# Where a two-level weight product takes its block sums from: sums that grow in place in DRAM, another order of v's seven products, and v's weights split in halves

## The chip, the cores and the metric

The kernel runs on one core of one Trainium2 chip. The metric is device time in microseconds (us) of one execution. Five engines work from queues of their own: TensorE (PE, matrix products), VectorE (DVE), ScalarE (ACT), GpSimd (POOL) and SyncE (SP, which here only issues DMAs). POOL issues DMAs too, and the copies with an addition that this text is about are all POOL's.

## The reference

One layer on x (512 tokens, 2048 channels), float32. What matters here are two of its products:

```python
h = _rmsnorm(x, g_pre)
proj = h @ w_in                       # q | k | v | z_att | u | g_glu | z_conv, 1024 columns each
q, k, v, z_att, u, g_glu, z_conv = jnp.split(proj, IN_SPLITS, axis=-1)
y_att = _stick_breaking_attention(q, k, v) * jax.nn.silu(z_att)
y_conv = _conformer_conv(u, g_glu, conv_w, conv_b, ln_g, ln_b, w_pw2, b_pw2) * jax.nn.silu(z_conv)
y = jnp.concatenate([y_att, y_conv], axis=-1) @ w_out
out = x + _rmsnorm(y, g_post)
```

## The kernel before

Every float32 operand of a product is split in two parts of a shorter type: `hi` on ACT and `lo` = source minus `hi` on DVE (`split`, L96). A product is then three matmuls (hi·hi, hi·lo, lo·hi).

The program is a list of steps. A step loads one 1 MB block of weights (SP, into a `raw` buffer), splits it, and runs two units on PE. For q, k, u and the gates a step is half of the 2048 rows of 256 columns: 48 matmuls. For v a step is 24 matmuls. `raws`, `his` and `los` have two buffers each. So the load for a step can start when the split of the step two before it has ended, and a split can start when PE has left the `hi` and `lo` of the step two before it.

Two of the products, v (L532 to L649) and the output projection (L831 to L972), use a scheme with seven products in place of eight. The weight matrix is cut into 2 x 2 blocks (r, c). Products 1, 3 and 2 use a plain block, products 5, 6, 7 and 4 a sum of blocks, and seven "forms" of the activations (sums and differences of blocks of h, made by `make_v_form` on DVE and split on ACT and DVE) stand on the other side. Sum 5 is (0,0)+(0,1), sum 6 is sum 5 + (1,1), sum 4 is sum 6 + (1,0), sum 7 is (0,1)+(1,1). Each block and sum has two halves by rows, kg 0 and 1; below, "5.0" is product 5, half 0, and so on. v has 14 such steps of one pair, w_out 28 of two pairs.

The sums are made in DRAM by POOL's DMA queue (`plan_sums`, L492): a copy of the base (L506), then a copy of another block that is added to it (L502, `accum_op`). Both are put in a queue, `v_sumq` or `sumq`, and `sum_next` (L514) takes the next one at fixed places of the program: one behind each of the later blocks of the first stage, then one behind each unit of a step (v), or one per step from step 18 on (w_out). `sum_next` makes the DMA wait for the last matmul issued so far by the functions that record it (`latest`).

In v the order of products is `V_ORDER = (1, 2, 5, 6, 3, 7, 4)`. The forms are made when a certain step's weights are loaded: `{(1, 0): 5, (2, 1): 6, (6, 1): 3, (3, 0): 7}` (L614). Instructions carry priorities. PE keeps the order of the program text; ACT, DVE, POOL and SP get a fixed order in which the scheduler placed them by priority. Between v's splits on DVE stand the taps of the convolution (L396, L401: `acc`, 31 for each of two channel tiles at this time), whose priority is low; POOL has, in one queue with the sums, a MEMSET of a convolution buffer (L392: `hg`) that waits until the 31 taps of an earlier tile are done.

## Time and profile before

| what | value |
|---|---|
| time, median of 3 runs | 870.19 us (869.29 to 872.12) |
| time of the profiled execution | 871.51 us, of which its span (first to last instruction) is 869.8 us |
| mean granted TensorE clock | 0.997 |
| PE, DVE, ACT, POOL busy | 98%, 73%, 45%, 14% of the span |
| DMA queue of SP (q1) | 110.12 MB, 37.3% of 16 engines' span |
| DMA queue of POOL (q0) | 52.43 MB, 26.1% |
| v's sums: copies from w_in (L502 and L506) | 12 of 1 MB, median 12.9 us to landing |
| v's sums: copies of sums | 4 of 1 MB, median 12.7 us |
| w_out's sums: copies from w_out, copies of sums | 24, median 9.3 us; 8, median 5.3 us |

A row of the timeline reads: start in us, length in us, engine, line and operation, tile written and tiles read, shapes, number of merged instructions, and in brackets the idle time of the engine before it and what ended that. Matmuls overlap: the time that one takes is seen from start to start.

### The profile page before, as it was taken

How to read it: one execution, taken by the hardware profiler on the slowest of the kernel's cores; microseconds unless marked ns; L12 is line 12 of the kernel's file. 1: busy time of each engine (PE TensorE's matmuls, PEld its weight loads, DVE VectorE, ACT ScalarE, POOL GpSimd, SP SyncE). 2: the span in 40 equal slices, each digit the busy share in tenths (PEclk: the TensorE clock that was granted, in tenths of full speed). 3: DMA queues.
4: the chain of work that ended last, by engine and by line, in shares of the span. 5: the costliest groups of instructions: out<-in, count | busy, mean ns of one | idle time of the engine just before them, and what ended most of it. 6: DMA issues, size and time to landing. Idle time of an engine off the chain costs nothing.

```text
span 869.8 us, 9834 instructions
## 1 busy us (share of the span) xinstructions
PE 855.0 (98%) x3894; PEld 710.0 (82%) x3894; DVE 631.0 (73%) x773; ACT 395.3 (45%) x452; POOL 124.5 (14%) x154
## 2 busy tenths in 40 slices
PE   9999998999999999999999999999999999999995
PEld 7888787888888888888888888888888888888884
DVE  4798799986797979879696984245643776458775
ACT  5785124644443544243422545235722346455542
POOL 0221100001202132203111323031001000000031
PEclk9999999999999999999999999999999999999998
DMA  8899964568578455874488547862232346556783
GB/s 324 250 272 283 281 158 160 185 207 302 173 181 174 165 193 145 179 189 165 145 192 165 176 157 183 175 162 97 93 101 97 98 154 233 194 194 250 289 279 101
DMA packets 87046, 163.58 MB, mean 188 GB/s; under 512 B 3014, under 2 KB 52434, under 8 KB 83224
## 3 DMA queue, kind: packets, MB, share of 16 engines
q1 hardware_dynamic: 69824, 110.12, 37.3%
q0 software_dynamic: 16864, 52.43, 26.1%
q8 instruction: 30, 0.49, 0.2%
q10 hardware_dynamic: 312, 0.40, 0.1%
q14 instruction: 16, 0.13, 0.0%
HBM read 158.75 MB, written 54.53 MB: 245 GB/s over the span
## 4 chain that ended last, share of the span: by engine, by line
PE 80%; DVE 10%; DMA 6%; ACT 2%; issue 1%; POOL 0%; DVEq 0%; ACTq 0%; POOLq 0%
PE za L342 3%; PE zc L342 3%; PE za L344 3%; PE a L940 3%; PE zc L344 3%; PE za L343 3%; PE a L942 3%; PE zc L343 3%; PE a L941 3%; DVE acc L401 3%; DVE l_v L100 3%; DMA r_k<-in_w_in_dram 3%; PE k L342 3%; PE q L344 3%; PE q L342 3%; PE u L344 3%
## 5 line engine op out<-in xcount | busy, mean ns | idle before, releaser
L401 DVE SCALAR_TENSOR_TENSOR acc<-hg,vec,acc 128x512 f32<-128x512 f32 x240 | 182.2, 759 | 6.8
L100 DVE TENSOR_TENSOR l_w<-r_w,h_w 128x2048 fp32r<-128x2048 f32 x28 | 64.1, 2291 | 41.9 <-ACT h_w L99 41.9
L99 ACT ACTIVATE h_w<-r_w 128x2048 fp32r<-128x2048 f32 x28 | 53.5, 1915 | 42.1 <-DMA r_w<-ws 11.8
L344 PE MATMUL k<-h_hi,l_k 128*128 128x512 f32 x128 | 50.1, 391 | 1.1 <-DVE l_k L100 1.1
L342 PE MATMUL u<-h_hi,h_u 128*128 128x512 f32 x128 | 50.3, 393 | 0.0
L342 PE MATMUL q<-h_hi,h_q 128*128 128x512 f32 x128 | 50.1, 392 | 0.0
L342 PE MATMUL k<-h_hi,h_k 128*128 128x512 f32 x128 | 50.0, 391 | 0.0
L342 PE MATMUL za<-h_hi,h_za 128*128 128x512 f32 x128 | 50.0, 390 | 0.0
L342 PE MATMUL zc<-h_hi,h_zc 128*128 128x512 f32 x128 | 49.9, 390 | 0.0
L344 PE MATMUL u<-h_hi,l_u 128*128 128x512 f32 x128 | 49.9, 390 | 0.0
L344 PE MATMUL q<-h_hi,l_q 128*128 128x512 f32 x128 | 49.9, 390 | 0.0
L344 PE MATMUL za<-h_hi,l_za 128*128 128x512 f32 x128 | 49.8, 389 | 0.0
L344 PE MATMUL zc<-h_hi,l_zc 128*128 128x512 f32 x128 | 49.8, 389 | 0.0
L343 PE MATMUL u<-h_lo,h_u 128*128 128x512 f32 x128 | 49.8, 389 | 0.0
L343 PE MATMUL k<-h_lo,h_k 128*128 128x512 f32 x128 | 49.8, 389 | 0.0
L343 PE MATMUL za<-h_lo,h_za 128*128 128x512 f32 x128 | 49.8, 389 | 0.0
L343 PE MATMUL q<-h_lo,h_q 128*128 128x512 f32 x128 | 49.8, 389 | 0.0
L343 PE MATMUL zc<-h_lo,h_zc 128*128 128x512 f32 x128 | 49.8, 389 | 0.0
L940 PE MATMUL a<-h_w,f_hi 128*128 128x512 f32 x128 | 49.8, 389 | 0.0
L941 PE MATMUL a<-l_w,f_hi 128*128 128x512 f32 x128 | 49.8, 389 | 0.0
L942 PE MATMUL a<-h_w,f_lo 128*128 128x512 f32 x128 | 49.8, 389 | 0.0
L671 POOL TENSOR_SCALAR_AFFINE_SELECT t<-t 128x128 f32<-128x128 f32 x64 | 35.7, 635 | 81.1 <-DVE t L694 48.2
(339 smaller groups left out, 2136.7 us busy)
## 6 DMA issues: line engine op xcount, KB each, us to landing
ws<-in_w_out_dram POOLq DMA_DIRECT2D x24, 1024.0 KB, 9.3
r_w<-ws SPq DMA_DIRECT2D x16, 1024.0 KB
vs<-in_w_in_dram POOLq DMA_DIRECT2D x12, 1024.0 KB, 12.9
r_w<-in_w_out_dram SPq DMA_DIRECT2D x12, 1024.0 KB
r_u<-in_w_in_dram SPq DMA_DIRECT2D x8, 1024.0 KB
r_q<-in_w_in_dram SPq DMA_DIRECT2D x8, 1024.0 KB
r_k<-in_w_in_dram SPq DMA_DIRECT2D x8, 1024.0 KB
r_v<-vs SPq DMA_DIRECT2D x8, 1024.0 KB
```

The source lines that it names most:

```text
L99: nc.scalar.activation(hi, src, AF.Copy)
L100: nc.vector.tensor_tensor(out=lo, in0=src, in1=f32(hi), op=ALU.subtract)
L342: nc.tensor.matmul(ps, wh, ah, start=first, stop=False)
L343: nc.tensor.matmul(ps, wh, al, start=False, stop=False)
L344: latest[0] = nc.tensor.matmul(ps, wl, ah, start=False, stop=last).ins
L401: bgq.append(lambda j=j: nc.vector.scalar_tensor_tensor(out=acc, in0=hg[:, j : j + S], scalar=vec[:, ct, j : j + 1], in1=acc, op0=ALU.mult ...
L671: nc.gpsimd.affine_select(out=blk, in_=blk, compare_op=ALU.is_gt, fill=0.0, base=0, pattern=[[-1, P]], channel_multiplier=1,)
L940: nc.tensor.matmul(ps, fh[:, kk, ts], hi[:, k, :], start=st, stop=False, skip_group_check=True)
L941: nc.tensor.matmul(ps, fh[:, kk, ts], lo[:, k, :], start=False, stop=False, skip_group_check=True)
L942: nc.tensor.matmul(ps, fl[:, kk, ts], hi[:, k, :], start=False, stop=en, skip_group_check=True)
```

## The change

- `plan_sums` makes whole copies only for the sums named in `fresh`. The others grow in place: when the load of sum 5 (or 6) has been issued, an added copy into the same DRAM tile is queued, which turns it into sum 6 (or 4). For v the fresh sums are 5 and 7, so 6 and 4 grow; for w_out they are 5, 6 and 7, and 4 grows from 6. Of v's 16 copies 12 are left, of w_out's 32 are 28.
- w_out's growing copies have a queue of their own, `grow`, from which one is taken behind every unit; v's go into `v_sumq`.
- `V_ORDER` becomes (5, 1, 2, 6, 3, 7, 4). Form 5 is made at the step two before v's first, and the other forms at other loads.
- v's weights are split as two halves of 1024 columns (`split_halves`): two instructions on ACT and two on DVE for each block, in place of one and one.

```diff
+    def split_halves(hi, lo, src):
+        half = src.shape[1] // 2
+        for a in (0, half):
+            split(hi[:, a : a + half], lo[:, a : a + half], src[:, a : a + half])
...
-    def plan_sums(name, order, pairs, block):
+    def plan_sums(name, fresh, pairs, block):
         made, todo = {}, deque()
+        def take_up(q, p, kg):
+            return nc.gpsimd.dma_start(made[q, p, kg], block(*SUMS[q][1], p, kg), accum_op=ALU.add)
+        def begin(q, p, kg):
+            base = SUMS[q][0]
+            made[q, p, kg] = dram.tile([P, 4, S], F32, name=f"{name}{q}{p}{kg}")
+            return nc.gpsimd.dma_start(
+                made[q, p, kg],
+                made[base, p, kg] if isinstance(base, int) else block(*base, p, kg),
+            )
+        for q in fresh:
+            for f in (begin, take_up):
                 for p in range(pairs):
                     for kg in range(2):
+                        todo.append(partial(f, q, p, kg))
+        grown = {SUMS[q][0]: q for q in (6, 4) if q not in fresh}
+        def loaded_sum(q, p, kg, queue):
+            if q in grown:
+                made[grown[q], p, kg] = made[q, p, kg]
+                queue.append(partial(take_up, grown[q], p, kg))
+        return made, todo, loaded_sum
...
-    V_ORDER = (1, 2, 5, 6, 3, 7, 4)
+    V_ORDER = (5, 1, 2, 6, 3, 7, 4)
-    v_sum, v_sumq = plan_sums("vs", (5, 6, 7, 4), 1, v_w)
+    v_sum, v_sumq, v_loaded = plan_sums("vs", (5, 7), 1, v_w)
...
-            split(hi, lo, raw)
-        form = {(1, 0): 5, (2, 1): 6, (6, 1): 3, (3, 0): 7}.get((q, kg))
+            split_halves(hi, lo, raw)
+        v_loaded(q, 0, kg, v_sumq)
+        form = {(1, 1): 6, (6, 0): 3, (3, 0): 7}.get((q, kg))
...
-    w_sum, sumq = plan_sums("ws", (5, 6, 4, 7), 2, w_block)
+    w_sum, sumq, w_loaded = plan_sums("ws", (5, 6, 7), 2, w_block)
+    grow = deque()
...
+        w_loaded(q, p, kg, grow)
...
+        if n == n_v - 2:
+            with tc.high_priority(offset=LATER):
+                make_v_form(5)
...
             sum_next(v_sumq)
+            sum_next(grow)
```

The change moves instructions at three places. The first is DVE at the start of product u, 58 to 70 us in the trace: `whole` is the first quarter of the normalised input, `h_lo_120` its low part, which PE reads piece by piece, and the lines L555 and L569 begin form 5. Before:

```order
L280 SCALAR_TENSOR_TENSOR whole<-whole,g_col,rbc 128x512
L308 TENSOR_TENSOR h_lo_121<-xw_1_430,h_hi_117 128x4x128
L280 SCALAR_TENSOR_TENSOR whole<-whole,g_col,rbc 128x512
L308 TENSOR_TENSOR h_lo_120<-whole,h_hi_116 128x512
L280 SCALAR_TENSOR_TENSOR whole<-whole,g_col,rbc 128x512
L308 TENSOR_TENSOR h_lo_120<-whole,h_hi_116 128x512
L280 SCALAR_TENSOR_TENSOR xw_2_465<-xw_2_465,g_col,rbc 128x128 x4
L308 TENSOR_TENSOR h_lo_120<-whole,h_hi_116 128x512
L280 SCALAR_TENSOR_TENSOR xw_2_502<-xw_2_502,g_col,rbc 128x128 x4
L308 TENSOR_TENSOR h_lo_120<-whole,h_hi_116 128x512
```

And of the changed kernel, at the same place:

```order
L285 SCALAR_TENSOR_TENSOR whole<-whole,g_col,rbc 128x512
L313 TENSOR_TENSOR h_lo_121<-xw_1_430,h_hi_117 128x4x128
L569 TENSOR_TENSOR xw_3_664<-xw_1_377,xw_3_664 128x512
L569 TENSOR_TENSOR xw_3_693<-xw_1_430,xw_3_693 128x512
L285 SCALAR_TENSOR_TENSOR whole<-whole,g_col,rbc 128x512
L313 TENSOR_TENSOR h_lo_120<-whole,h_hi_116 128x512
L285 SCALAR_TENSOR_TENSOR whole<-whole,g_col,rbc 128x512
L313 TENSOR_TENSOR h_lo_120<-whole,h_hi_116 128x512
L285 SCALAR_TENSOR_TENSOR xw_2_465<-xw_2_465,g_col,rbc 128x128 x4
L313 TENSOR_TENSOR h_lo_120<-whole,h_hi_116 128x512
L285 SCALAR_TENSOR_TENSOR xw_2_502<-xw_2_502,g_col,rbc 128x128 x4
L313 TENSOR_TENSOR h_lo_120<-whole,h_hi_116 128x512
```

The two additions of form 5 have moved ahead of all four pieces of `h_lo_120`; before, they stood behind them.

The second place is POOL's queue of copies for v's sums (`vs`). L506 begins a sum, L502 adds to it. Before, behind the first four (sum 5 begun and completed):

```order
L506 DMA vs_537<-vs_379 16x16384
L506 DMA vs_568<-vs_432 16x16384
L502 DMA vs_537<-in_w_in_dram 512x1x512
L502 DMA vs_568<-in_w_in_dram 512x1x512
L506 DMA vs_666<-in_w_in_dram 512x1x512
L506 DMA vs_697<-in_w_in_dram 512x1x512
L502 DMA vs_666<-in_w_in_dram 512x1x512
L502 DMA vs_697<-in_w_in_dram 512x1x512
L506 DMA vs_845<-vs_537 16x16384
L506 DMA vs_881<-vs_568 16x16384
L502 DMA vs_845<-in_w_in_dram 512x1x512
L502 DMA vs_881<-in_w_in_dram 512x1x512
```

And of the changed kernel, behind the same four (L508 begins, L503 adds):

```order
L508 DMA vs_537<-in_w_in_dram 512x1x512
L508 DMA vs_568<-in_w_in_dram 512x1x512
L503 DMA vs_537<-in_w_in_dram 512x1x512
L503 DMA vs_568<-in_w_in_dram 512x1x512
L397 MEMSET hg_1932 128x30
L503 DMA vs_379<-in_w_in_dram 512x1x512
L503 DMA vs_432<-in_w_in_dram 512x1x512
L503 DMA vs_379<-in_w_in_dram 512x1x512
L503 DMA vs_432<-in_w_in_dram 512x1x512
```

Sum 7 now comes right behind sum 5, and the tiles of sum 5 (`vs_379`, `vs_432`) are added to twice more, behind the MEMSET: the first two rows make sum 6, the last two sum 4. By the program each waits for the load of the sum before (5.0, 5.1, 6.0, 6.1) and for PE's first unit of the step ahead of that load's own: k's last step, 5.0, 2.1 and 6.0.

The third place is DVE at the start of v, 127 to 152 us in the trace: `l_v` is the low part of a block of v's weights, `acc` the taps. Before (the first four blocks are 1.0, 1.1, 2.0, 2.1):

```order
L100 TENSOR_TENSOR l_v_1120<-r_v_1118,h_v_1119 128x2048
L100 TENSOR_TENSOR k_lo_1169<-k_0_1061,k_hi_1168 128x512
L396 TENSOR_SCALAR acc_914<-hg_911,vec 128x512
L401 SCALAR_TENSOR_TENSOR acc_914<-hg_911,vec,acc_914 128x512 x8
L100 TENSOR_TENSOR l_v_1210<-r_v_1208,h_v_1209 128x2048
L100 TENSOR_TENSOR k_lo_1201<-k_1_1090,k_hi_1200 128x512
L401 SCALAR_TENSOR_TENSOR acc_914<-hg_911,vec,acc_914 128x512 x3
L100 TENSOR_TENSOR l_v_1244<-r_v_1242,h_v_1243 128x2048
L401 SCALAR_TENSOR_TENSOR acc_914<-hg_911,vec,acc_914 128x512 x5
L100 TENSOR_TENSOR l_v_1280<-r_v_1278,h_v_1279 128x2048
```

And of the changed kernel (the first four blocks are 5.0, 5.1, 1.0, 1.1):

```order
L100 TENSOR_TENSOR l_v_1128<-r_v_1126,h_v_1127 128x1024 x2
L100 TENSOR_TENSOR k_lo_1159<-k_0_1069,k_hi_1158 128x512
L401 TENSOR_SCALAR acc_904<-hg_901,vec 128x512
L406 SCALAR_TENSOR_TENSOR acc_904<-hg_901,vec,acc_904 128x512 x6
L100 TENSOR_TENSOR l_v_1201<-r_v_1199,h_v_1200 128x1024 x2
L100 TENSOR_TENSOR k_lo_1192<-k_1_1098,k_hi_1191 128x512
L406 SCALAR_TENSOR_TENSOR acc_904<-hg_901,vec,acc_904 128x512 x4
L100 TENSOR_TENSOR l_v_1238<-r_v_1236,h_v_1237 128x1024 x2
L406 SCALAR_TENSOR_TENSOR acc_904<-hg_901,vec,acc_904 128x512 x4
L100 TENSOR_TENSOR l_v_1276<-r_v_1274,h_v_1275 128x1024 x2
```

Each `l_v` is two instructions now, and six taps in place of eight stand ahead of the second block's.

## The prediction

> **What bounds the kernel now.** I read the engines' busy times first, then who PE waited for, then PE's rows around each wait, then what was late there.

> ```profile
> PE 855.0 (98%) x3894; PEld 710.0 (82%) x3894; DVE 631.0 (73%) x773; ACT 395.3 (45%) x452; POOL 124.5 (14%) x154
> ```

> The waits of PE, from the table of waits (sum, count, largest):

> ```profile
> PE va L635 <- DVE l_v L100: 2.4, 1, 2.4
> PE idle L1123 <- POOL mean_w L134: 1.8, 1, 1.8
> PE k L344 <- DVE l_k L100: 1.1, 1, 1.1
> PE va L634 <- ACT v_a L596: 0.4, 1, 0.4
> ```

> PE is the bound from end to end, and it waits four times. The second wait is at the program's start, where nothing changes. So the change can win at most the other three; everything else that it saves (12 of 16 copies left in v, 28 of 32 in w_out) is off the path. Since matmuls overlap, a wait is read from start to start:

> ```profile
> 155.10 0.39 PE L634 MATMUL vb<-h_v,vf_00h 128*128 128x512 f32 x1
> 165.98 0.39 PE L634 MATMUL va<-h_v,vf_00h 128*128 128x512 f32 x1
> ```

> These are the starts of products 5 and 6, 48 matmuls apart: 10.88 / 48 = 0.227 us each, 5.44 a step of v, 2.72 a unit. The rows around the three waits:

> ```profile
> 135.92 0.39 PE L634 MATMUL va<-h_v,h_hi 128*128 128x512 f32 x1
> 138.72 0.50 PE L635 MATMUL va<-l_v,h_hi 128*128 128x512 f32 x1 [2.41 <-DVE l_v L100]
> ...
> 107.19 0.39 PE L343 MATMUL k<-h_lo,h_k 128*128 128x512 f32 x1
> 108.68 0.50 PE L344 MATMUL k<-h_hi,l_k 128*128 128x512 f32 x1 [1.11 <-DVE l_k L100]
> ...
> 201.27 0.39 PE L636 MATMUL va<-h_v,h_lo 128*128 128x512 f32 x1
> 202.03 0.50 PE L634 MATMUL va<-h_v,h_hi 128*128 128x512 f32 x1 [0.38 <-ACT v_a L596]
> ```

> Beyond that pace the waits cost 2.57 (v, at block 1.1), 1.26 (k) and 0.53 (v, at 4.1), and each is followed by one matmul of 0.50 in place of 0.39. That makes 2.7, 1.4 and 0.6: 4.7 us in all, 0.5% of the time.

> **What was late there.** For k it was a load of weights; for v the order on DVE:

> ```profile
> 82.38 0.37 SPq L327 DMA_DIRECT2D r_k<-in_w_in_dram  x1
> 104.39 1.92 ACT L99 ACTIVATE h_k<-r_k 128x2048 fp32r<-128x2048 f32 x1 [17.24 <-DMA r_k<-in_w_in_dram]
> 106.34 2.29 DVE L100 TENSOR_TENSOR l_k<-r_k,h_k 128x2048 fp32r<-128x2048 f32 x1 [4.44 <-ACT h_k L99]
> ```

> On POOL's queue at that time:

> ```profile
> 83.68 1.57 POOL L506 DMA_DIRECT2D vs<-vs  x2
> 101.43 1.18 POOL L502 DMA_DIRECT2D vs<-in_w_in_dram  x1 [16.18 <-DMA vs<-vs]
> 104.33 1.16 POOL L502 DMA_DIRECT2D vs<-in_w_in_dram  x1 [1.72 <-DMA vs<-vs]
> ```

> And on DVE ahead of v's second block:

> ```profile
> 130.20 6.26 DVE L401 SCALAR_TENSOR_TENSOR acc<-hg,vec,acc 128x512 f32<-128x512 f32 x8
> 136.38 2.28 DVE L100 TENSOR_TENSOR l_v<-r_v,h_v 128x2048 fp32r<-128x2048 f32 x1
> ```

> k's load took 22.0 us (82.38 to 104.39), beside POOL's copies, and DVE stood 4.4 us for it. At v's second block PE waited to 138.72 for an `l_v` that began only when eight taps were done.

> **k's wait goes: -1.4.** In the changed order sum 7 follows sum 5 at once, and nothing more is copied until v. The copies issued from 83.68 on, which made sum 4, are gone there, and r_k loads alone. How long a load takes alone, and how long beside copies, shows elsewhere:

> ```profile
> 712.51 0.38 SPq L862 DMA_DIRECT2D r_w<-in_w_out_dram  x1
> 717.90 1.92 ACT L99 ACTIVATE h_w<-r_w 128x2048 fp32r<-128x2048 f32 x1 [0.68 <-DMA r_w<-in_w_out_dram]
> ...
> 108.66 0.37 SPq L612 DMA_DIRECT2D r_v<-in_w_in_dram  x1
> 121.25 1.92 ACT L99 ACTIVATE h_v<-r_v 128x2048 fp32r<-128x2048 f32 x1 [9.97 <-DMA r_v<-in_w_in_dram]
> ```

> An added copy alone, from the list of DMA issues (the one at 234.80; the last number is us to landing):

> ```profile
> ws<-in_w_out_dram POOLq DMA_DIRECT2D x1, 1024.0 KB, 9.0
> ```

> A block of 1 MB with rows of 512 columns lands in 5.4 us alone (712.51 to 717.90) and in 12.6 us (108.66 to 121.25) beside the two added copies of 101.43 and 104.33. An added copy alone takes 9.0 us. At 5.4 to 12.6 us after 82.38 r_k is there before 95, and `l_k` need not wait. Cost between nothing and a loss is excluded: the copies are gone from that stretch.

> **v's wait at the second block goes: -2.7.** Six taps in place of eight stand before it: two taps less are 2 x 6.26 / 8 = 1.6 us. The 4.4 us for which DVE stood at `l_k` bring DVE forward too, as far as PE lets it. And PE needs only the first half of `l_v` to start. 1.6 us alone leave 1.0 of the wait; with the first half at about 1.1 us in place of 2.2 it is gone, whatever comes of the 4.4.

> **4.1's wait goes: -0.6.** ACT's copy `v_a` stood behind a chain of splits that was late by a load; with halves DVE's part is ready earlier. Kept, it costs 0.6: both ends.

> **The halves.** From here come their prices:

> ```profile
> 126.83 2.28 DVE L100 TENSOR_TENSOR l_v<-r_v,h_v 128x2048 fp32r<-128x2048 f32 x1
> 129.03 0.68 DVE L100 TENSOR_TENSOR k_lo<-k,k_hi 128x512 fp32r<-128x512 f32 x1
> ```

> Two of 512 in a row:

> ```profile
> 171.53 0.69 DVE L100 TENSOR_TENSOR vf_00l<-xw,vf_00h 128x512 fp32r<-128x512 f32 x1
> 172.13 0.69 DVE L100 TENSOR_TENSOR vf_01l<-xw,vf_01h 128x512 fp32r<-128x512 f32 x1
> ```

> DVE's next row starts 2.20 us after one of 2048 elements and 0.60 after one of 512: (2.20 - 0.60) / 1536 x 1024 + 0.067 = 1.13 us for a half, so a split block costs 14 x 0.07 = 1.0 us more over all of v, beside PE's 76 us. ACT's half is about 1.0 (half of 1.92 and a little). From a load's landing to the first half of `l_v` I count 2.2 us in place of some 4.2.

> [...]

> **New at the start: +0.8.** Form 5's two additions now stand ahead of `h_lo_120`, whose last piece PE reads soon after it is made:

> ```profile
> 66.38 0.68 DVE L308 TENSOR_TENSOR h_lo<-whole,h_hi 128x512 fp32r<-128x512 f32 x1
> ...
> 68.63 1.28 DVE L555 TENSOR_TENSOR xw<-xw,xw 128x512 f32<-128x512 f32 x2
> 69.83 2.28 DVE L100 TENSOR_TENSOR l_u<-r_u,h_u 128x2048 fp32r<-128x2048 f32 x1
> ```

> and PE's first matmul with that piece:

> ```profile
> 67.58 0.39 PE L343 MATMUL u<-h_lo,h_u 128*128 128x512 f32 x1
> ```

> The two take 69.83 - 68.63 = 1.20 us, and no gap on DVE ahead of them takes that up. The last piece then ends at 67.06 + 1.20 = 68.26 and PE's L343 starts at about 68.31 in place of 67.58: 0.73, and 0.1 for the slow matmul behind. The earlier three pieces still come in time (each is read 0.68 us before the next, and they are made 1.25 to 1.66 us apart). Between 0 (if DVE has slack that I don't see) and 0.9.

> **New in v: the sums that grow beside v's loads: +4.0.** Before, no copy ran during v. Now four added copies do, issued behind PE's first unit of k's last step, of 5.0, 2.1 and 6.0. The steps run 5.0, 5.1, 1.0, 1.1, 2.0, 2.1, 6.0, 6.1, 3.0, 3.1, ... A load is issued when the split of the step two before ends. How far ahead that is, before:

> ```profile
> 165.62 0.38 SPq L612 DMA_DIRECT2D r_v<-in_w_in_dram  x1
> ```

> This is the ninth step's load; its step starts two steps after 165.98 (product 6's start, above), at 176.86, so it leads by 11.2 us. Alone, 5.4 + 4.2 for the whole split fit.

> The ninth step is now 3.0, a plain block. The copies that make sum 4 are issued 2.72 us into step 2.1, which is 3 x 5.44 - 2.72 = 13.6 us before 3.0 starts, and 2.72 into 6.0, 8.2 us before. At 9.0 us each alone, one behind the other in one queue, they run through the whole 11 us of this load. That is the state of the load at 108.66: 12.6 us. With 2.2 for the first half, less the 0.2 by which PE needs `lo` later than `hi`: 12.6 + 2.2 - 0.2 - 11.2 = **3.4** us of wait, 0.1 for the matmul behind it. Bounds: 0 if it loads as alone; some 8 if it lands only when both copies are through (two of 9.0 from 13.6 us before the step end 4.4 after it, stretched by the load's own 2 to 3, then 2.2). I take the value of the nearest row, which has two such copies too.

> The copy for 6.1 meets the load of 1.1 in the same way. There DVE is ahead (4.4 us no longer stood, two taps less), the load leads by some 13 us, and only one copy is beside it: 0.5, between 0 and 1.8 (12.6 + 2.2 - 13).

> What hides the rest: the loads of 6.0, 6.1, 7.0 and on come from contiguous sums or when no copy runs. POOL's MEMSET stands ahead of the first growing copy, but waits for taps that DVE ends before v; what is queued behind the copies there, the next MEMSET, is needed after v.

> **w_out: 0.** Its four growing copies go out as the loads of 6 land, about 740 to 757 us, and the loads of products 6 and 3 meet them. A third `hi`/`lo` buffer makes these loads lead by more; I see 0, and 2 at worst for the first plain block behind.

> **The sum.** -2.7 - 1.4 - 0.6 + 0.8 + 3.5 + 0.5 = +0.1 us. Against the profiled execution's 871.51 us this is 871.6; against the median of 870.19, which the comparison uses, **870.3**.

> **The rivals.**
> - *The loads land in time* (the copies leave SP's queue its share). For it: a single copy is through in 9.0, less than the lead. Against: the load at 108.66. Then 870.2 - 4.7 + 0.8 = 866.3.
> - *Slower: the two copies hold the load of 3.0 until they are through*, 8 in place of 3.4, with 1.1's load late by 1.8. For it: k's load at 22.0 us under a longer row of copies. It decides from a load of about 15 us on: 870.3 + 4.6 + 1.3 = 876; from 14.5 us on, the total is beyond 872.8.
> - *The change doesn't free k's load*, because the copies of sum 7, now earlier, still run at 82. For it: they wait for each other's landing. Then the 1.4 stay: 871.7.

> **How the numbers follow.** The forecast, a gain and a loss that cancel to within 2.6 us, has 0.47; the loads in time 0.25; the copies holding them 0.24; k's load not freed 0.04. A measurement of this kernel tells 0.3%, 2.6 us, from no change. So faster by more than that 0.25, within 0.51, slower 0.24. The range goes from the first rival's 866.3 to 874.5, which is a load of 3.0 of some 16 us; what lies beyond is less than 2 in 10.

> **What would show it.** In the profile of the changed kernel: no wait of PE for `l_k` and none at the second block of v; a wait of 0.7 us for `h_lo` near 68 us; `h_v` waiting for the DMA of the ninth block, near 175 us, and PE behind it for 3 to 4 us; POOL's copies of 6 and 4 inside v. I am wrong if the ninth block's load takes under 9 us, or if PE waits elsewhere for more than 1 us.

## The result, and the profile after

| | before | changed | ratio, 95% interval |
|---|---|---|---|
| median, us | 870.59 (6 runs) | 880.26 (6 runs) | 1.0118 (1.0086 to 1.0151) |
| profiled execution, us | 871.51 | 882.42 | |
| its span, us | 869.8 | 880.7 | |

The changed kernel is 1.2% slower. The forecast was no change. PE is still the bound, 97% in place of 98%:

```profile
PE 858.6 (97%) x3894; PEld 711.0 (81%) x3894; DVE 632.5 (72%) x787; ACT 396.0 (45%) x466; POOL 120.5 (14%) x146
```

PE's busy time is 3.6 us more and the span 10.9 us: for most of the loss PE stands and waits. PE's waits, from the table of waits of the changed kernel (sum, count, largest):

```profile
PE b L958 <- DVE l_w L100: 3.1, 2, 1.6
PE a L958 <- DVE l_w L100: 2.5, 3, 1.8
PE vb L649 <- ACT h_v L99: 2.4, 1, 2.4
PE idle L1140 <- POOL mean_w L139: 1.8, 1, 1.8
PE vb L650 <- DVE l_v L100: 1.0, 2, 0.8
PE va L649 <- ACT v_a L610: 0.8, 1, 0.8
PE a L957 <- ACT h_w L99: 0.7, 1, 0.7
PE u L348 <- DVE h_lo L313: 0.6, 1, 0.6
```

The old waits at k and at v's second block are gone. What is new in v and at the start was forecast; the rows with `l_w` and `h_w` were not: they are w_out, where PE did not wait at all before. The same waits from start to start, in PE's timeline of the changed kernel:

```profile
173.22 0.39 PE L651 MATMUL va<-h_v,vf_11l 128*128 128x512 f32 x1
175.97 0.50 PE L649 MATMUL vb<-h_v,vf_00h 128*128 128x512 f32 x1 [2.36 <-ACT h_v L99]
177.22 0.50 PE L650 MATMUL vb<-l_v,vf_00h 128*128 128x512 f32 x1 [0.76 <-DVE l_v L100]
...
202.38 0.39 PE L651 MATMUL va<-h_v,h_lo 128*128 128x512 f32 x1
203.52 0.50 PE L649 MATMUL va<-h_v,h_hi 128*128 128x512 f32 x1 [0.75 <-ACT v_a L610]
...
774.86 0.39 PE L957 MATMUL b<-h_w,f_hi 128*128 128x512 f32 x1
776.74 0.50 PE L958 MATMUL b<-l_w,f_hi 128*128 128x512 f32 x1 [1.50 <-DVE l_w L100]
...
782.09 0.39 PE L957 MATMUL b<-h_w,f_hi 128*128 128x512 f32 x1
784.07 0.50 PE L958 MATMUL b<-l_w,f_hi 128*128 128x512 f32 x1 [1.59 <-DVE l_w L100]
...
858.57 0.39 PE L959 MATMUL a<-h_w,f_lo 128*128 128x512 f32 x1
859.62 0.50 PE L957 MATMUL a<-h_w,f_hi 128*128 128x512 f32 x1 [0.66 <-ACT h_w L99]
861.94 0.79 PE L958 MATMUL a<-l_w,f_hi 128*128 128x512 f32 x1 [1.82 <-DVE l_w L100]
862.53 0.63 PE L959 MATMUL a<-h_w,f_lo 128*128 128x512 f32 x1
```

Take 0.227 off each distance. Step 3.0 then costs 2.52 + 1.02 and 0.1 for the slow matmul behind, 3.65 in all. In w_out two waits stand in the middle, 1.65 and (behind 782.09) 1.75, 3.6 with what follows them. Behind 840 us come 0.57, 0.45, 0.82 and 2.09, and after the last some six matmuls at 0.43 us each, 5.6 in all. That is 9.2 of the 10.9 us between the two profiled executions. Counted at the same matmul of both kernels, PE is 1.4 us later where w_out begins, 5.0 behind its middle and 10.8 at the end, so that w_out costs 9.4.

What was late there, first the four growing copies on POOL:

```profile
741.34 1.18 POOL L503 DMA_DIRECT2D ws<-in_w_out_dram  x1 [69.92 <-DMA r_w<-ws]
750.00 1.15 POOL L503 DMA_DIRECT2D ws<-in_w_out_dram  x1 [7.49 <-DMA r_w<-ws]
756.19 1.16 POOL L503 DMA_DIRECT2D ws<-in_w_out_dram  x1 [5.03 <-DMA r_w<-ws]
762.40 1.16 POOL L503 DMA_DIRECT2D ws<-in_w_out_dram  x1 [5.06 <-DMA r_w<-ws]
```

and a plain block of product 3, its load on SP's queue and its split on ACT:

```profile
766.49 0.38 SPq L878 DMA_DIRECT2D r_w<-in_w_out_dram  x1
```

```profile
779.78 1.92 ACT L99 ACTIVATE h_w<-r_w 128x2048 fp32r<-128x2048 f32 x1 [4.94 <-DMA r_w<-in_w_out_dram]
```

The copies go out as each load of 6 lands, 6.2 to 8.7 us apart, closer together than the 9.0 us that one takes alone, and the load of 766.49 takes 13.3 us, where one alone took 5.4 (712.51 to 717.90, before). Before, ACT's splits of this block (768.26) and of the one ahead of it waited for PE to leave a buffer, not for a load:

```profile
762.82 1.92 ACT L99 ACTIVATE h_w<-r_w 128x2048 fp32r<-128x2048 f32 x1 [2.13 <-PE a L942]
...
768.26 1.92 ACT L99 ACTIVATE h_w<-r_w 128x2048 fp32r<-128x2048 f32 x1 [3.05 <-PE a L942]
```

Those waits were a part of the loads' lead, the time by which a load is there before it is needed. The last load of weights shows what became of it, on SP's queue of before and of the changed kernel:

```profile
839.72 0.33 SPq L862 DMA_DIRECT2D r_w<-ws  x1
```

```profile
850.01 0.33 SPq L878 DMA_DIRECT2D r_w<-ws  x1
```

It goes out 10.3 us later, while PE at 843 us was only some 5.0 later (1.4 up to w_out, 3.6 in its middle). Five us of lead are gone, and the last three loads, which are split 6.9 to 7.9 us after their issue beside the stores of the output in both kernels, now come late.

### The profile page after: what moved, and what is told of

The parts are those of the page before. It is cut to its first block, busy times and chain, and to the rows that moved or that the text cites. A ratio compares the mean times of both kernels' runs of the same rounds, so it can differ in the third digit from the quotient of the medians.

```text
span 880.7 us, 9844 instructions
## 1 busy us (share of the span) xinstructions
PE 858.6 (97%) x3894; PEld 711.0 (81%) x3894; DVE 632.5 (72%) x787; ACT 396.0 (45%) x466; POOL 120.5 (14%) x146
## 4 chain that ended last, share of the span: by engine, by line
PE 72%; DVE 12%; DMA 10%; ACT 4%; issue 2%; POOL 0%; DVEq 0%; ACTq 0%; POOLq 0%
DMA r_w<-ws 5%; PE za L347 3%; PE q L348 3%; PE zc L349 3%; PE q L349 3%; PE za L348 3%; PE za L349 3%; PE zc L347 3%; PE q L347 3%; PE zc L348 3%; PE u L348 3%; PE u L349 3%; PE u L347 3%; PE k L347 3%; PE k L348 3%; PE k L349 3%
## 5 line engine op out<-in xcount | busy, mean ns | idle before, releaser
L100 DVE TENSOR_TENSOR l_w<-r_w,h_w 128x2048 fp32r<-128x2048 f32 x28 | 64.1, 2292 | 51.9 <-ACT h_w L99 51.8
L99 ACT ACTIVATE h_w<-r_w 128x2048 fp32r<-128x2048 f32 x28 | 53.5, 1914 | 53.2 <-DMA r_w<-ws 25.4
## 6 DMA issues: line engine op xcount, KB each, us to landing
ws<-in_w_out_dram POOLq DMA_DIRECT2D x24, 1024.0 KB, 9.2
r_w<-ws SPq DMA_DIRECT2D x16, 1024.0 KB
vs<-in_w_in_dram POOLq DMA_DIRECT2D x12, 1024.0 KB, 11.8
r_w<-in_w_out_dram SPq DMA_DIRECT2D x12, 1024.0 KB
r_u<-in_w_in_dram SPq DMA_DIRECT2D x8, 1024.0 KB
r_q<-in_w_in_dram SPq DMA_DIRECT2D x8, 1024.0 KB
r_k<-in_w_in_dram SPq DMA_DIRECT2D x8, 1024.0 KB
r_v<-vs SPq DMA_DIRECT2D x8, 1024.0 KB
```

The source lines that it names most:

```text
L99: nc.scalar.activation(hi, src, AF.Copy)
L100: nc.vector.tensor_tensor(out=lo, in0=src, in1=f32(hi), op=ALU.subtract)
```

## The experiments

Theory W: the growing copies of w_out cost the time, first by late loads, then by the lead that is used up. Rival V: the late loads of v cost it. Every edit below is to the changed kernel, unless it says otherwise. Numbers in brackets are the 95% interval of the ratio to before.

**e1: w_out's sum 4 copied whole again.**

```diff
-    w_sum, sumq, w_loaded = plan_sums("ws", (5, 6, 7), 2, w_block)
+    w_sum, sumq, w_loaded = plan_sums("ws", (5, 6, 4, 7), 2, w_block)
```

> The changed kernel, but w_out's sum 4 is copied whole ahead of time as before; v as changed. Theory W (the growing copies of w_out cost the time: PE stands 3.6 us near 775 to 784 us, the lead of the loads is used up, and another 5.6 us follow at the end): no wait of PE at w_out, and what is left is v's and the start's balance, about +1.2 us against before: 871 to 872.5 us. Rival V (v's late loads shift the whole program, and the end stands for that reason): 878 us or more, with PE's waits behind 840 us still there.

872.31 us, 1.0033 (1.0021 to 1.0044). PE waits nowhere in w_out, though v's late loads are still there (2.15 us from start to start at 3.0). That is theory W.

**e2: before, with w_out's sum 4 grown and nothing else** (v's order, sums, forms and splits as before).

```diff
-    V_ORDER = (5, 1, 2, 6, 3, 7, 4)
+    V_ORDER = (1, 2, 5, 6, 3, 7, 4)
-    v_sum, v_sumq, v_loaded = plan_sums("vs", (5, 7), 1, v_w)
+    v_sum, v_sumq, v_loaded = plan_sums("vs", (5, 6, 7, 4), 1, v_w)
-            split_halves(hi, lo, raw)
+            split(hi, lo, raw)
...
```

The part left out makes the forms at the same loads as before.

> The kernel before, but w_out's sum 4 grows from sum 6 as in the changed kernel; v, its order, its splits and its sums as before. Theory W: the same two groups of PE's waits, about 3.6 us near 775 us and 4 to 6 us behind 840 us, so 878 to 880 us. Rival V: 870 to 872 us.

878.60 us, 1.0106 (1.0086 to 1.0126). Both groups of waits are there, in its table of waits:

```profile
PE b L958 <- DVE l_w L100: 2.9, 2, 1.8
...
PE a L958 <- DVE l_w L100: 1.8, 1, 1.8
```

So w_out alone costs about 1.1%, and what is left in e1 is 0.3%: together 1.4%, inside the interval of the whole change (0.9 to 1.5%).

**e3: the four copies one for every two steps.** (In the changed kernel the call behind every unit holds nothing back: `latest` isn't updated in w_out.)

```diff
-                nc.tensor.matmul(ps, fl[:, kk, ts], hi[:, k, :], ...)
+                latest[0] = nc.tensor.matmul(ps, fl[:, kk, ts], hi[:, k, :], ...).ins
...
-            sum_next(grow)
+            if n % 2 == 0 and unit is step.units[0]:
+                sum_next(grow)
```

> The changed kernel, but each of w_out's four growing copies waits for a later unit of PE: one for every two steps (10.9 us), from about 758 us on. Theory crowding (four copies one right behind the other, as the loads of 6 land, hold a row of loads; one copy alone is hidden by the lead of the loads): PE's waits near 775 us under 0.5 us and at the end under 2 us, 871 to 875 us. Rival (every added copy beside a load of 2 KB rows takes its share whatever the spacing, and the lead doesn't come back): 877 us or more.

880.61 us, 1.0143 (1.0108 to 1.0177), as the rival says. The copies went out at 755.86, 766.74, 777.62 and 788.50, and took 8.9 to 11.2 us. The waits in the middle fell to one of 0.95, but at the end all are there:

```profile
PE a L958 <- DVE l_w L100: 3.2, 3, 1.8
...
PE a L957 <- ACT h_w L99: 0.6, 1, 0.6
```

My theory of crowding falls: spread out, the copies cost no less, and the lead goes either way. That the time which loads spend beside an added copy decides is my reading of the two runs; it was not tested by itself.

**e4: before, without w_out's third hi/lo buffer, and without a growing copy.**

```diff
-        if turn[0] % 3 == 0:
+        if turn[0] < 0:
```

> The kernel before, with two hi/lo buffers in w_out in place of three, and no growing copy: the loads' lead is taken away by other means. Theory lead (the waits behind 840 us in the changed kernel come from loads of 7 to 7.5 us beside the stores of the output, which only the third buffer's lead hides): PE waits 2 to 6 us behind 830 us, none near 775 us, 872 to 877 us. Rival (the waits at the end come from the growing copies themselves or from POOL's queue): no wait, 870 to 871 us.

879.04 us, 1.0099 (1.0073 to 1.0126). The lead theory holds, though the loss is above its range:

```profile
PE a L941 <- DVE l_w L100: 3.8, 3, 1.8
...
PE a L940 <- ACT h_w L99: 1.1, 1, 1.1
```

The waits behind 830 us come without any copy, once the lead is gone. Part of what is above the range is TensorE's clock (last section).

**e11: the same four copies, without the addition.**

```diff
-            return nc.gpsimd.dma_start(made[q, p, kg], block(*SUMS[q][1], p, kg), accum_op=ALU.add)
+            extra = {} if name == "ws" and q == 4 else dict(accum_op=ALU.add)
+            return nc.gpsimd.dma_start(made[q, p, kg], block(*SUMS[q][1], p, kg), **extra)
```

This kernel leaves out the sum: product 4 of w_out gets a plain block, and the output is not the layer's.

> The changed kernel, but w_out's four growing copies write over the block of sum 6 in place of adding to it (product 4 of w_out gets block (1,0) in place of its sum; v is as changed): the same 4 MB, at the same places, without the addition. Theory add (an added copy holds the DMA engines longer: 9.0 us alone, a plain copy 5.3): the loads of 6 and 3 beside them take 6 to 9 us in place of 7.5 to 13.2, PE's wait near 775 us is under 1 us and at the end under 3 us, 871.5 to 876 us. Rival (any copy of rows of 2 KB beside loads does it): 878 us or more.

872.35 us, 1.0014 (1.0000 to 1.0027), and no wait in w_out. Below is, from the summary of DMAs between 740 and 770 us, of the changed kernel and of this one, first POOL's queue (packets, MB, share of 16 engines), then its issues (KB, median us to landing):

```profile
q0 software_dynamic: 1630, 3.24, 60.3%
...
ws<-in_w_out_dram POOLq DMA_DIRECT2D x4, 1024.0 KB, 14.9
```

```profile
q0 software_dynamic: 1088, 4.19, 37.1%
...
ws<-in_w_out_dram POOLq DMA_DIRECT2D x4, 1024.0 KB, 8.3
```

The adding copies hold the 16 DMA engines for 60.3% of these 30 us for 3.24 MB, the plain ones for 37.1% for 4.19: 5.6 against 2.7 us of all 16 engines per MB. Their neighbours show it: product 3's first two loads are split 7.9 us after their issue here, and 12.2 and 13.3 us after it there. The addition makes the loss, not the 4 MB that are copied.

**e5: v's copies that make sum 4 issued later**, beside the contiguous loads of 7 (w_out as in e1).

```diff
-        v_loaded(q, 0, kg, v_sumq)
+        v_loaded(q, 0, kg, v_sumq if q == 5 else v_late)
...
+            if n >= n_v + 7:
+                sum_next(v_late)
```

> w_out's sums copied whole as in e1_w_whole, and v's two copies that make sum 4 issued later: behind PE's first and second unit of step 6.1 in place of the first units of 2.1 and 6.0, so that they run beside the contiguous loads of product 7 and not beside the plain loads of product 3. Theory Q (the late loads of 3.0 and 3.1, and with them the waits at 3.0, 3.1, 7.0 and 4.1, come from those two copies alone): the loads of 3.0 and 3.1 take 5 to 7 us, PE's 3.8 us of waits at 3.0 to 7.0 are gone and 4.1's falls to 0.6 or less: 872.3 - 3.8 - 0.8, 867 to 868.8 us. Rival D (DVE has no slack from step 2.0 on, the split of 3.0 is late anyhow): 870.5 us or more, with PE waiting for l_v at 3.0. Rival M (the wait moves: 4.0 or 7.0 waits for the sum or for a load beside the copies): a wait of 1 us or more there, 869.5 to 872 us.

873.06 us, 1.0025 (1.0013 to 1.0037), above the times of Q and of M. The loads of 3.0 and 3.1 take 4.9 and 4.8 us and PE doesn't wait there, so Q is right on the cause; but the wait moves, as M says. The next waits are

```profile
PE va L650 <- ACT v_a L611: 3.4, 2, 2.2
```

because the second copy, issued at 173.76, lands at 193.74, and the load of 4.1 goes out only then (193.81). Neither of the two places that were tried for these copies is free of a wait.

**e6: e5, with form 5 later** (`offset=LATER` becomes `offset=200` at its call).

> e5_v4_late, and form 5 is made at a lower priority, so that its additions stand on DVE behind all pieces of h_lo_120 as before the change. Theory Q: PE's wait for h_lo near 67 us (0.75 and 0.1 behind it) goes, 0.85 us less than e5_v4_late: 866.2 to 868 us. Rival: form 5 comes late at v's start or takes DVE's time from k, and PE waits there for 1 us or more: 868 us or more.

872.63 us, 1.0019 (1.0009 to 1.0029), not the 866 to 868 that I expected. PE's wait near 67 us is gone from the profile, and PE reaches product 4 of v 0.9 us earlier (193.95 against 194.84); 4.1 waits as in e5. The medians of e5 and e6 are 0.4 us apart and their intervals cover each other, so the times don't tell whether that 0.9 us is won.

**e7: e6, with whole splits** (`split_halves` becomes `split`).

> e6_v4_late_f5, but v's weights are split whole, as before the change, in place of halves. Theory (at v's second block the two taps less and DVE's 4.4 us no longer stood take the wait away; the halves matter only where a load is late): within 1 us of e6_v4_late_f5, no wait at the second block. Rival (the halves took that wait away): 2 us or more above e6_v4_late_f5, with PE waiting for l_v at the second block.

872.97 us, 1.0031 (1.0019 to 1.0043): within 1 us, as expected, and nothing at the second block. But the profile has 4.3 us of waits for `l_v` (e6: 0.4), the first at 1.1, whose load runs beside a copy:

```profile
PE va L651 <- DVE l_v L100: 4.3, 3, 1.8
```

In this profile, then, the halves pay where a load is late, while 4.1 waits less (0.9 in place of 2.4). But the profiled execution took 875.03 us, one of four of the ten at 874.6 to 875.5; the other six took 872.5 to 873.1, and e6's median is 872.63. That the halves pay is not shown by the times.

**e8: all sums of v whole too**, with the new order and the halves kept.

```diff
-    v_sum, v_sumq, v_loaded = plan_sums("vs", (5, 7), 1, v_w)
+    v_sum, v_sumq, v_loaded = plan_sums("vs", (5, 6, 7, 4), 1, v_w)
```

> w_out's sums copied whole as in e1_w_whole and v's sums all copied ahead too, in the order 5, 6, 7, 4 as before; the new order of v's products and the halves stay. Theory: k's wait for l_k is back (1.1 to 1.5 us), for the copies of 4 are back beside k's load; no wait in v at 1.1 or at 3.0 to 7.0; the start's 0.85 stays: 866.5 to 869 us. Rival (v's order makes 3.0 late by itself): PE waits 2 us or more at 3.0 and the time is 870.5 us or more.

868.97 us, 0.9977 (0.9964 to 0.9990): faster than before. PE doesn't wait at 3.0, so the order of products doesn't make it late; it waits 1.5 us at 4.1, and at k 0.24 in place of the 1.1 to 1.5 that I expected. With no sum growing, the rest of the change (order, forms and halves) is a gain of 0.2%.

**e9 and e10: the copies `v_a` ahead of `h_v` on ACT; then form 5 later as well.**

```diff
-            nc.scalar.copy(ps, v_ps[q, i])
+            with tc.high_priority(offset=1500):
+                nc.scalar.copy(ps, v_ps[q, i])
```

> e8_v_all_whole, and ACT's copies v_a (the banks of product 7) get a higher priority, so that the second stands ahead of the two halves of h_v for step 4.1 and not behind them. Theory order (PE's wait at 4.1 comes from that place in ACT's queue, and neither from the halves nor from a growing copy): the wait of 1.5 us goes, 1.3 to 1.6 us less than e8_v_all_whole, 867 to 868 us; against before a ratio of about 0.996. Rival (PE waits for something else there, or h_v comes late in its place): no gain, and a wait at 4.0 or 4.1.

> e9_va_first, and form 5 at the lower priority, which takes PE's wait for h_lo near 67 us away. Theory cover (in e8_v_all_whole the wait at the start was paid back at k, where PE waits for a load that lands when it lands: 1.26 us before the change, 0.24 with the start 0.85 later): the wait at k grows to 1.0 to 1.3 us, and the time is within 0.4 us of e9_va_first. Rival (the start's wait is a cost of its own): 0.85 us less than e9_va_first.

869.23 us, 0.9971 (0.9959 to 0.9983), and 869.97 us, 0.9975 (0.9962 to 0.9989). Both are above what was expected of e9, 867 to 868 us, for the wait at 4.1 stayed, 1.57 us. DVE's timeline of e9, and POOL's:

```profile
196.40 2.50 DVE L617 TENSOR_TENSOR v_part<-v_part,v_a 128x512 f32<-128x512 f32 x1
```

```profile
196.93 1.41 POOL L420 TENSOR_TENSOR ln_sum<-acc,acc 128x512 f32<-128x512 f32 x1
```

The second `v_a` stands behind a `v_hi` that waits for this `v_part`, and `v_part` took 2.50 in place of 0.68. So e9 does not settle theory order: ahead of `h_v` the second `v_a` saves the some 1.9 us that ACT spent on `h_v`, and the slower `v_part` takes 1.8 of them back.

In e10 the start's wait is gone and k waits 1.30, as "cover" says; but e12 has both waits, and e2 and e4, the same as before up to k, have none at k. Its load lands between 102.7 and 105.6 us in these profiles, so k's wait is in some of these executions and not in others. "Cover" is not shown.

**e12: both copies `v_a` one behind the other**, product 7's subtractions behind the second (added to e8).

```diff
+            if i == 0:
+                v_ps["held"] = ps
+                return
+            tt(out=v_part[5, 0], in0=v_part[5, 0], in1=v_ps["held"], op=ALU.subtract)
+            v_keep(1, 2, v_part[5, 0])
```

> e8_v_all_whole, and ACT makes both copies v_a one behind the other, ahead of v_hi and of the halves of h_v for step 4.1 (product 7's two subtractions and splits follow behind the second). Theory chain (PE's 1.5 us at 4.1 in e8_v_all_whole and e9_va_first come from the chain v_a, DVE's v_part, ACT's v_hi, v_a, in which the second v_a waits for DVE): PE's wait at 4.1 is under 0.4 us, 1.1 to 1.6 us less than e8_v_all_whole: 867.3 to 868.2 us, ratio to before about 0.996. Rival (what DVE loses beside POOL's addition ln_sum near 197 us, 2.50 us for an operation of 0.69 in e9_va_first, makes l_v of 4.1 late): a wait for l_v of 1 us or more at 4.1, the time as e8_v_all_whole.

868.11 us, 0.9976 (0.9963 to 0.9989). Its table of waits has no `v_a` any more:

```profile
PE idle L1146 <- POOL mean_w L139: 1.8, 1, 1.8
PE k L349 <- DVE l_k L100: 1.1, 1, 1.1
PE u L348 <- DVE h_lo L313: 0.6, 1, 0.6
```

So the second `v_a` was late for what stood between the two copies on ACT: `v_hi`, which waits for DVE, and in e8 `h_v` too. The edit takes both away and doesn't tell them apart. That 1.5 us less doesn't show in the ratio: the intervals of e8, e9, e10 and e12 cover each other. Each of the four is 0.2 to 0.3% faster than before, and none is told from the others.

## Why the prediction was wrong

The step that failed is **"w_out: 0 ... I see 0, and 2 at worst"**. It measured 9.2 us (3.6 and 5.6); the other terms together came to +1.7 in place of +0.1. The prediction's own sign of being wrong came true with it: PE waits elsewhere, in w_out, for more than 1 us. By the prediction's own terms, in the profiled executions:

| term | forecast | measured |
|---|---|---|
| k | -1.4 | -1.4 |
| v's second block | -2.7 | -2.7 |
| 4.1 | -0.6 | +0.4 (1.0 in place of 0.6) |
| start, `h_lo` | +0.8 | +0.9 |
| load of 3.0 | +3.5 | +3.6 |
| load of 1.1 | +0.5 | 0 |
| 3.1 and 7.0, behind it | not counted | +0.9 |
| w_out | 0 | +9.2 |
| sum | +0.1 | +10.9 |

Counted at the same matmuls, w_out has 9.4 and all ahead of it 1.4; the rows leave out small differences, a second wait of 0.3 us at k among them.

- **The mechanism was known and priced, but for v only.** A load of rows of 512 columns beside added copies was put at 12.6 us, and the load of 3.0 took 13.4 (161.50 to 174.86). The same meeting in w_out was named, and dismissed with the third buffer's lead. It should have been walked like v: four copies of 9 us or more are at least 36 us in one queue, the time of six loads, each late by up to 8 us, against a lead that the wait of ACT's splits for PE shows in part (2.1 and 3.1 us for one block and the next, before).
- **A lead is a stock, not a cover for each load.** PE waited only 3.6 us beside the copies; the rest came 60 us later, beside the stores, which no growing copy touches. e4 shows these waits with the lead taken away by other means, e3 with copies that hardly make PE wait where they run. Why the loads don't win the lead back between 785 and 838 us wasn't tried. The trace has a hint: ACT's splits at 805.67 and 827.30 stand right behind `jy` (L892), work on the output for which ACT had just waited 4.76 and 3.02 us, so that a load which lands early may not be split early.
- **The rival on the slower side** (the copies hold the load of 3.0 until they are through) had the direction right, but not the reason: the load took 13.4 us, not 15, and e1, where v's copies still grow, is only 0.3% slower than before. Its bound of some 8 us was added up too low, too: 4.4, 2 to 3 and 2.2 are 8.6 to 9.6.
- **4.1** was argued from the halves. e12 shows ACT's order instead: behind the first `v_a` stand a `v_hi`, which waits for DVE's `v_part`, and `h_v`, and only then the second `v_a`. With the halves the wait stayed.
- **k** was right in the two profiles compared, but its 1.4 us are one execution's: e2 and e4, the same as before up to k, don't have them.
- **The halves** cost PE nothing that these profiles show, as forecast: e7, which splits whole, has the more waits for `l_v` (4.3 us against 0.4 in e6), and the times of e6 and e7 (872.63 and 872.97 us) don't differ clearly.

## What to carry to other kernels

A transfer saved off the critical path gained nothing here; where the remaining ones ran cost 1.1%. Before an added copy is moved next to loads that something waits for, count its DMA time (here 5.6 us of all engines per MB) against the whole lead that these loads have, up to the end of the program. A stage without waits is not a stage with room: read what its splits waited for.

## What was not expected of the hardware

- **The clock after a wait.** Of 14 waits of PE of 2.0 us or more in these profiles, 9 were followed, at once or a few matmuls later, by up to nine matmuls 0.2 us too long, 1.5 to 1.7 us in all (waits from start to start, less 0.227). The granted clock says why. e4 by stretches: us, busy time of PE, PEld, DVE, ACT and POOL, then the clock, the DMA share and GB/s:

```profile
135.20:138.20 3.00, 0.56 (x3) 0.17 (x2) 3.00 (x3) 1.91 (x1) 0.00 (x0) 1.00 0.00 0
138.20:142.00 3.80, 3.80 (x10) 2.95 (x11) 3.73 (x5) 0.00 (x0) 0.00 (x0) 0.55 0.74 244
138.55:141.96 3.41, 3.41 (x9) 2.65 (x9) 3.34 (x5) 0.00 (x0) 0.00 (x0) 0.50 0.81 267
```

Before, after the same wait of 2.57 us at the same place, the next stretch reads

```profile
138.80:142.50 3.70, 3.70 (x16) 3.04 (x17) 3.63 (x5) 0.59 (x1) 0.00 (x0) 1.00 0.71 217
```

So one wait costs 2.7 us in one execution and 4.3 in another.

The clock records of these traces show when. The half clock lasts 3.41 us each of the 9 times, and it begins a whole number of such windows after the record's first change to the full clock (in e4 that is 12.26 us, and 37 windows later 138.55; in the changed kernel 11.49, and 249 windows later 861.41). In the window ahead of each of the 9 drops PE stood for 2.2 to 3.2 us in all (what starts are apart beyond 0.227), and in no other window between 30 us and PE's last matmul for more than 1.9. In e4 the wait of 2.60 us lies whole in one window; before, an edge at 136.97 cuts the same wait, and some 1.8 us fall to the larger part.

- **DVE beside POOL.** In e9 an addition on POOL of 1.41 us (196.93) came with a DVE subtraction that lasted 2.50 in place of 0.68, and in the changed kernel one of 1.40 (`ln_sum`, 201.02) with a subtraction of 1.85 (`v_lo`, 201.13) in place of 0.69. In e12 the subtraction of 198.44 took 2.30. What makes them longer was not tried. In POOL's queue `ln_sum` stands behind the first of w_out's copies in e9 (196.93) and behind the second before (206.02), when no such subtraction runs.
